# A streaming encoder step: TensorE's order written out by stages as generators, attention staggered by one key tile, x placed tile by tile

## The chip, the cores and the metric

The kernel runs on one core of a Trainium2 chip. A core has five engines, each with its own in-order queue: TensorE (PE, matrix products and transposes through it), VectorE (DVE), ScalarE (ACT), GpSimd (POOL) and SyncE (SP), which here issues all the DMAs. The metric is the device time of one launch in microseconds, the median of three runs.

## The reference, cut to what matters

One layer of a hybrid encoder is applied to a prompt of 2048 tokens (batch 1, no past) and to 64 new tokens of a running stream (the "sample", with 2048 past keys). The model width is 1024.

```python
proj = x @ w_in                       # 1024 x 3856, split among four mixers of 4 heads x 64
o_a  = gated_delta(conv(q, k, v), beta, g)    # recurrence over chunks, triangular solve per chunk
o_b  = stick_breaking(q, k_all, v_all)        # attention; weights below
o_c  = sigmoid(gate) * mlstm(q, k, v, i, f)   # recurrence with a stabiliser
o_d  = hgrn2(silu(q), k, v, log_f)            # recurrence, gate per channel
mix  = (rmsnorm(concat(o_a, o_b, o_c, o_d)) * gates) @ w_out
x    = layernorm(alpha * x + mix)
x    = layernorm(alpha * x + square(relu(x @ w1 + b1)) @ w2 + b2)   # w1: 1024 x 4096

# stick breaking, per head and query block
z     = q @ k.T / 8
log1m = where(kpos < qpos, log_sigmoid(-z), 0)
after = reverse_cumsum(log1m) - log1m         # sum over all later keys
a     = where(kpos < qpos, exp(log_sigmoid(z) + after), 0)
o     = a @ v
```

All is float32. The outputs are y for both sequences, the new keys and values, and the states of the three recurrences.

## The kernel before, in words

**Tiling.** Tokens come in tiles of 128; the sample is one tile of 64. Four tiles make a block (`blocks`; block 0 also holds the sample tile), two tiles a unit (`units`, the piece of a block that the recurrences work on at once). For the MLP the sample tile goes with the last block (`mlps`).

**Products.** Every dense float32 operand is kept as a high and a low part, and `mm3` (L412) makes one product from three matmuls. `load_w` (L387) brings a weight group: at first use the raw weights are loaded, split by ACT (L405) and POOL (L406) and both parts are stored to DRAM; later uses load the parts. Six buffers each hold `whi` and `wlo`. `chan_mm` (L442) puts channels on the partitions (up to 512 tokens wide), `tok_major` (L453) tokens; each result has one of four PSUM buffers (`pd`) until ACT or DVE has taken it away. The transposed x of one block lies in `XH` and `XL` (single buffers). `load_T` (L431) loads a token tile in two halves into `x2` buffers (a ring of six, which the evacuations of the projections use as well) and `split_T` (L423) transposes it by PE, copies the high part by ACT (L428) and the low part by DVE (L429).

**Stages.** `project(b)` (L493) places all tiles of a block, then runs the steps of `w_in` in a list: the queries of attention (`SBQ`), its keys and values (`SBK`, `SBV`), gates, the delta mixer's q, k, v, and so on; results go to DRAM. `ev_k` (L534) also transposes each tile's keys right after the product (L541). `attention(b)` (L1194) goes through the four heads, and for each through the key tiles backwards. A round is two matmuls for the scores (L1217, L1218), a bound by DVE (L1187, or L1190 on the diagonal), exp and ln by ACT (L1167, L1168), the sum of the later tiles added into one row by DVE (L1172), a high part by ACT (L1174) and a low part by POOL (L1175), two matmuls for the sums over keys (L1177, L1178), a subtraction by DVE (L1179), exp (L1180), high part (L1182), low part by DVE (L1183), and the matmuls with the values into `po` (L1224, L1225). Scores and sums share two PSUM buffers (`pa`). `attention_sample` (L1239) does the same for 64 queries over the 16 past key tiles and its own. `gates`, `gdn`, `mlstm` and `hgrn` work a unit off, with one PSUM buffer for the first two (`ps`) and one for the others (`ph`). `mix` (L1353) multiplies the normalised outputs `t.o` by `w_out`, adds x and makes the first layer norm; the result goes to DRAM as `x1`. `mlp(b)` (L1400) runs 16 slices of 256 hidden channels, `up` and one slice later `down` (L1442).

**What sets the order.** The program text goes block by block: `project`, `attention`, the unit's mixers; after the last projection the MLPs. The mixes of the first MLP's tokens stand between the last projection's steps 12 and 16 (`MIX_0`), those of the next MLP's tokens after slices 8 and 12 of the MLP before (`MIX_AT`), and `start` (L1389) places the next MLP's x after its last `up`. A planner then orders the instructions of every engine: it plays the program through with its own costs and lets each engine take, of what is ready, what stands first in the text. So matmuls of attention and recurrences come to lie between those of later projections and MLPs, where the planner thought their operands ready. On the chip each engine follows the planned list in order.

Of the kernel before, what the change touches and what calls it, by code (L numbers as in the profile page):

```python
# [13 lines left out]
P = 128  # L14
# [11 lines left out]
R_X2 = 6  # L26
MIX_AT = (8, 12)
# [26 lines left out]
def encoder_step(ctx: ExitStack, tc: tile.TileContext, a, o):  # L54
# [135 lines left out]
    def move(dst, src):  # L190

        SP.dma_start(dst if dst.dtype == F32 else dst.bitcast(F32), src if src.dtype == F32 else src.bitcast(F32))

# [188 lines left out]

    split = {}
# [47 lines left out]
    def load_T(t, off, src):  # L431

        for g in range(2):
            xt = x2([P, 512])
            SP.dma_start(xt[: t.n], src[:, 512 * g : 512 * g + 512])
            cs = slice(off, off + t.n)
            split_T(xt, t.n, XH[:, 4 * g : 4 * g + 4, cs], XL[:, 4 * g : 4 * g + 4, cs])

# [3 lines left out]
    def chan_mm(gr, b, evac):  # L442
        for o0, n in b.cols:
            pt = pd([P, n])
            for k in range(KD):
                h, l = gr[k // 4]
                mm3(pt, h[:, k % 4, :], l[:, k % 4, :], *x_at(k, slice(o0, o0 + n)), k == 0, k == KD - 1)
            evac(o0, n, pt)

    def chan_major(b, w, c0, evac):  # L450
        chan_mm(chan_w(w, c0), b, evac)
# [18 lines left out]
    pair = [ar([P, 4, 2 * TS], F32R) for _ in range(2)]  # L470

    def natural(b, w, c0, n, evac):
        gr = [load_w(w, 256 * i, 2, c0, n) for i in range(4)]
        for t in b.tiles:
            cs = slice(t.off, t.off + t.n)
            part = []

            def into(pt, first, t=t, part=part):
                if not t.sample:
                    return evac(t, pt)  # L480
                if first:
                    part.append(x2([t.n, n]))
                    return ACT.copy(part[0], pt)
                DVE.tensor_tensor(part[0], part[0], pt, ALU.add)
                evac(t, part[0])
# [7 lines left out]
    def project(b, between={}):  # L493
        for t in b.tiles:
            load_T(t, t.off, t.x)
            if t.sample:
                cs = slice(t.off, t.off + t.n)
                for g in range(2):
                    ACT.copy(pair[g][:, :, 0 : t.n], XH[:, 4 * g : 4 * g + 4, cs].bitcast(F32))
                    POOL.tensor_copy(pair[g][:, :, t.n : 2 * t.n], XL[:, 4 * g : 4 * g + 4, cs].bitcast(F32))  # L500

        def ev_plain(dst, lo=None, hi=None):
# [31 lines left out]
        def ev_k(t, pt):  # L534
# [4 lines left out]
            tp = pd([P, 2, P])  # L539
            for g in range(2):  # L540
                PE.transpose(tp[:, g, : t.n], s[: t.n, g * P : (g + 1) * P], perm if t.n == P else ident[: t.n, : t.n])  # L541
            h = x2([P, 2, P], F32R)
            l = x2([P, 2, P], F32R)
            ACT.copy(h[:, :, : t.n], tp[:, :, : t.n])
            DVE.tensor_tensor(l[:, :, : t.n], tp[:, :, : t.n], h[:, :, : t.n].bitcast(F32), ALU.subtract)

            kk = t.u.kk[:, :, t.j * P : t.j * P + t.n].rearrange("(g i) p n -> i p g n", i=2)
            for i in range(2):
                move(kk[i, rows(i)], h[rows(i), :, : t.n])
                move(kk[i, rows(1 - i)], l[rows(i), :, : t.n])  # L550
# [16 lines left out]
        def nat(c0, n, ev):  # L567
            return [lambda: natural(b, w_in, c0, n, ev)]

        steps = (  # L570
            chan(C_SBQ, 2, ev_q)
            + nat(C_SBK, 256, ev_k)
            + nat(C_SBV, 256, ev_v)
            + nat(C_GATE_A, 264, ev_nat(lambda t: t.ga, 264, True))
# [7 lines left out]
            + nat(C_HGG, 256, ev_nat(lambda t: t.hgg, 256, True))  # L582
        )
        for i, f in enumerate(steps):
            f()
            if i in between:
                between[i]()
# [994 lines left out]
```

## Time and profile before

| | |
|---|---|
| time, median of 3 runs | 3439.55 us (3435.79 to 3444.12) |
| the profiled execution | 3441.77 us, its span 3440.1 us |
| TensorE busy, mean granted clock | 3193.1 us (93%), 0.958 |
| weight loads into TensorE | 2687.6 us (78%) |
| VectorE, ScalarE, GpSimd busy | 2248.2 us, 1355.5 us, 868.0 us |
| DMA moved | 735.66 MB, 214 GB/s on average |

The span runs from the first to the last instruction of one execution. A matmul counts as busy from its start until its result is written; matmuls overlap, so a busy TensorE can still be at half its clock. The granted clock is a share of full speed. In lists of instructions `d<-XH,whi` means that the tile `d` is written from `XH` and `whi`; a group's line ends with the idle time of its engine just before it and what ended that wait.

### The profile page before, as it was taken

Reading aid. Unit: us, or ns where it says so; the run is one execution under the profiler, and the core shown is the slowest. Engines: PE = TensorE matmul, PEld = TensorE weight load, DVE = VectorE, ACT = ScalarE, POOL = GpSimd, SP = SyncE. Lnnn points to the kernel's source line nnn. Section 1 sums busy time; section 2 is a strip of 40 time slices with the busy share of each in tenths; the row PEclk is TensorE's granted clock in tenths of the full one; section 3 lists DMA queues with packets and bytes.
Section 4 is the critical chain, followed back from the end, with each engine's and each line's share of the span. In section 5 each row is a group of like instructions: output and inputs, shape, how many; then the busy total and the mean of one; then the engine's idle time right before and its main releaser. Section 6 shows DMA issues by size and latency. Waiting matters only on the chain. (4 is left out here: it accounts for less than half of the span.)

```text
span 3440.1 us, 60484 instructions
## 1 busy us (share of the span) xinstructions
PE 3193.1 (93%) x20906; PEld 2687.6 (78%) x20906; DVE 2248.2 (65%) x5423; ACT 1355.5 (39%) x3186; POOL 868.0 (25%) x958
## 2 busy tenths in 40 slices
PE   8988898989899888988999899999999999999997
PEld 7987787878787777866877677787777888799986
DVE  2328647565865996788799798779846354564445
ACT  3225434443544455555565545445321111221111
POOL 4322212211222333445454532312201000010001
PEclk9998898999898999998999899999999999999999
DMA  7996565566666776775877675567767587665552
GB/s 231 303 323 183 173 205 188 171 183 202 184 188 203 237 251 219 228 229 169 275 263 255 222 230 180 172 197 219 238 235 260 193 281 243 217 232 165 163 164 81
DMA packets 581614, 735.66 MB, mean 214 GB/s; under 512 B 105864, under 2 KB 310588, under 8 KB 581308
## 3 DMA queue, kind: packets, MB, share of 16 engines
q1 hardware_dynamic: 581308, 731.79, 66.5%
q8 instruction: 166, 2.72, 0.3%
q14 instruction: 140, 1.15, 0.1%
HBM read 548.63 MB, written 182.94 MB: 213 GB/s over the span
## 5 line engine op out<-in xcount | busy, mean ns | idle before, releaser
L413 PE MATMUL d<-XH,whi 128*128 128x512 f32 (+1 forms) x1840 | 666.5, 363 | 11.2 <-DMA whi<-wsp 4.0
L415 PE MATMUL d<-XH,wlo 128*128 128x512 f32 (+1 forms) x1840 | 661.8, 360 | 2.0 <-POOL wlo L406 1.6
L414 PE MATMUL d<-XL,whi 128*128 128x512 f32 (+1 forms) x1840 | 663.0, 360 | 0.1
L1439 DVE TENSOR_TENSOR acc<-d,acc 128x512 f32<-128x512 f32 x564 | 384.9, 686 | 232.5 <-PE d L415 222.0
L413 PE MATMUL d<-whi,hh 128*128 128x512 f32 x992 | 402.6, 407 | 20.0 <-DVE as L1172 6.6
L413 PEld LDWEIGHTS d<-XH,whi 128*128 128x128 f32 x1840 | 351.0, 191 | 61.1 <-DMA whi<-wsp 4.3
L415 PE MATMUL d<-whi,hh 128*128 128x512 f32 x992 | 397.0, 400 | 0.0
L414 PE MATMUL d<-wlo,hh 128*128 128x512 f32 x992 | 395.9, 399 | 0.4 <-DMA wlo<-wsp 0.4
L415 PEld LDWEIGHTS d<-XH,wlo 128*128 128x128 f32 x1840 | 351.1, 191 | 51.4 <-POOL wlo L406 2.3
L1175 POOL TENSOR_TENSOR ar<-as,ar 128x512 fp32r<-128x512 f32 (+3 forms) x177 | 212.5, 1201 | 706.0 <-ACT ar L1174 563.3
L414 PEld LDWEIGHTS d<-XL,whi 128*128 128x128 f32 x1840 | 350.8, 191 | 47.0 <-DVE XL L429 0.4
L406 POOL TENSOR_TENSOR wlo<-raw,whi 128x512 fp32r<-128x512 f32 (+1 forms) x204 | 272.6, 1345 | 327.7 <-ACT whi L405 251.0
L1418 ACT ACTIVATE x<-d,cbig 128x512 f32<-128x512 f32 (+1 forms) x160 | 97.6, 610 | 597.6 <-PE d L415 574.5
L413 PE MATMUL d<-whi,XH 128*128 128x256 f32 (+1 forms) x1024 | 296.8, 298 | 20.7 <-DMA whi<-wsp 7.8
L414 PE MATMUL d<-wlo,XH 128*128 128x256 f32 (+1 forms) x1024 | 298.1, 294 | 5.3 <-POOL wlo L406 4.6
L415 PE MATMUL d<-whi,XL 128*128 128x256 f32 (+1 forms) x1024 | 297.2, 293 | 0.0
L1420 DVE CAST hh<-x 128x512 fp32r<-128x512 f32 (+1 forms) x160 | 75.7, 474 | 259.2 <-ACT x L1419 258.7
L413 PEld LDWEIGHTS d<-whi,hh 128*128 128x128 f32 x992 | 188.8, 190 | 69.3 <-DVE as L1172 8.2
L415 PEld LDWEIGHTS d<-whi,hh 128*128 128x128 f32 x992 | 189.2, 191 | 43.8
L414 PEld LDWEIGHTS d<-wlo,hh 128*128 128x128 f32 x992 | 189.6, 191 | 41.9 <-DMA wlo<-wsp 0.8
L413 PEld LDWEIGHTS d<-whi,XH 128*128 128x128 f32 x1024 | 198.1, 197 | 26.5 <-DMA whi<-wsp 8.5
L414 PEld LDWEIGHTS d<-wlo,XH 128*128 128x128 f32 x1024 | 201.1, 197 | 8.3 <-POOL wlo L406 5.2
(445 smaller groups left out, 6437.9 us busy)
## 6 DMA issues: line engine op xcount, KB each, us to landing
whi<-wsp SPq DMA_DIRECT2D x644, 256.0 KB
wlo<-wsp SPq DMA_DIRECT2D x644, 256.0 KB
wsp<-whi SPq DMA_DIRECT2D x196, 256.0 KB
wsp<-wlo SPq DMA_DIRECT2D x196, 256.0 KB
raw<-in_w_dram SPq DMA_DIRECT2D x128, 256.0 KB
raw<-in_w_in_dram SPq DMA_DIRECT2D x52, 256.0 KB
ak<-kk SPq DMA_DIRECT2D x80, 128.0 KB
ak<-vv SPq DMA_DIRECT2D x80, 128.0 KB
```

What stands on the lines that cost most here:

```text
L406: POOL.tensor_tensor(lo, raw, hi.bitcast(F32), ALU.subtract)
L413: PE.matmul(out, lhsT=lh, rhs=rh, start=start, stop=False)
L414: PE.matmul(out, lhsT=lh, rhs=rl, start=False, stop=False)
L415: PE.matmul(out, lhsT=ll, rhs=rh, start=False, stop=stop)
L1175: POOL.tensor_tensor(sl, sp, sh.bitcast(F32), ALU.subtract)
L1418: ACT.activation(r, pt, AF.Relu, bias=b1c(ff))
L1420: DVE.tensor_copy(h[:, f, cs], r)
L1439: lambda pt, first, acc=acc: DVE.tensor_tensor(acc, pt, acc, ALU.add),
```

## The change: what it does

TensorE's instructions are taken out of the planner's hands (`tc.manual_schedule`): they are issued in the order of the program text, and the text's order is made by generators. The other engines stay with the planner. Every stage (`project`, `gates`, `gdn`, `mlstm`, `hgrn`, both attentions, `mix`, `mlp`, `start`) yields before its next group of matmuls a pair: the TensorE time assumed for the group just issued, and the time assumed until the operands of the next are ready. `interleave` keeps a clock of its own, on which 12 matmuls of n columns are taken as 12 n x 0.00045 us. The dense chain (`dense`: projections, then MLPs, with the mixes inside) runs on; at least every 2.5 us of that clock, or when it has to wait, each of four other chains that is due gets one step: `places` (x into place), `delta` (gates and delta mixer), `memories` (mLSTM, HGRN2) and `attend` (attention). Marks (`flag`, `need`) hold a stage back until what it reads has been issued. Attention issues the next tile's scores right behind a tile's sums, and the tile's value matmuls after the next tile's sums; keys and values of a unit are fetched ahead of use. x is placed tile by tile, the next tile's load issued one tile ahead; a later block's tile goes into place once the last step of the projection before has used that token tile. The projection starts with keys and values, then queries, and the keys' transposes follow one tile later. Beside this: the delta mixer's convolution works on pairs of channel groups; the mixes load the outputs `t.o` by halves ahead of use; `pair` moves from the `ar` ring to the `oh` ring; some POOL memsets (`fill_in`) keep their place in the program's order.

```diff
+MM = 0.00045
+EVERY = 2.5
...
+    def interleave(main, others):
+        due = {id(g): 0.0 for g in [main] + others}
+        alive = [main] + others
+        last = 0.0
+        def step(g):
+            r = next(g, 0)
+            if r is None:
+                return False
+            if r == 0:
+                alive.remove(g)
+            else:
+                clock[0] += r[0]
+                due[id(g)] = clock[0] + r[1]
+            return True
+        while alive:
+            known = len(done)
+            moved = main in alive and due[id(main)] <= clock[0] and step(main)
+            if not moved or clock[0] - last >= EVERY:
+                for g in sorted([g for g in alive if g is not main and due[id(g)] <= clock[0]], key=lambda g: due[id(g)]):
+                    moved = step(g) or moved
+                    last = clock[0]
...
     def chan_mm(gr, b, evac):
...
                 mm3(pt, h[:, k % 4, :], l[:, k % 4, :], *x_at(k, slice(o0, o0 + n)), k == 0, k == KD - 1)
+                if k % 4 == 3 and k < KD - 1:
+                    yield 12 * n * MM, 0
             evac(o0, n, pt)
+            yield 12 * n * MM, 0
...
+    def into_place(b):
+        nxt = load_T(b.tiles[0], b.tiles[0].x)
+        for j, t in enumerate(b.tiles):
+            xt = nxt
+            if b.i:
+                yield from need("xfree", b.i, j)
+            yield from put_T(t, t.off, xt)
+            if j + 1 < len(b.tiles):
+                nxt = load_T(b.tiles[j + 1], b.tiles[j + 1].x)
...
+            flag("xt", b.i, j, after=1.0)
...
         steps = (
-            chan(C_SBQ, 2, ev_q)
-            + nat(C_SBK, 256, ev_k)
+            nat(C_SBK, 256, ev_k, before=lambda t: need("xt", b.i, b.tiles.index(t)))
             + nat(C_SBV, 256, ev_v)
+            + chan(C_SBQ, 2, ev_q)
...
+                yield 0, 4
+                z, carry, prev = scores(*its[0]), None, None
+                pe = 0.5
+                for x, (u, t) in enumerate(its):
+                    zc, sp = stick(z, bound_diag if u.b is b else bound_plain)
+                    sh, sl = add_carry(sp, carry)
+                    yield pe, 7
+                    carry = sums(sh, sl, lowk)
+                    if prev:
+                        add_up(*prev)
+                    if x + 1 < len(its):
+                        z = scores(*its[x + 1])
...
+                    prev = (x, u, t, *weights(zc, carry))
+                    carry = carry[0:1, :]
+                    pe = 1.4
+                yield pe, 4.5
+                add_up(*prev)
...
+    with tc.manual_schedule(engines={PE.engine}):
+        interleave(dense(), [places(), delta(), memories(), attend()])
```

The assumed waits of the other stages have the same form: in `gdn` up to 30 us (the solve's first step), in `hgrn` 25 us (the factors), in `gates` 20 us, else mostly 1.5 to 9 us.

More of the change, by code (lines that the diff above doesn't have):

```diff
@@ L1468, in mlp @@
             elif sb < ns - 1 or not end:
[L1469 to L1473 removed]
+                yield from down([sb - 1])
+            if g:
+                yield from mix(g, ld)
+        yield from down([ns - 2, ns - 1] if end else [ns - 1])
     zero = g2([64, 514])
```

401 lines of the change are left out of this document (269 added, 132 removed).

## The prediction

> **What bounds the kernel now.** I read the page's engine totals and slices first, then the busy time by stretches, then TensorE's waits, then single matmuls in the timeline.
>
> ```profile
> span 3440.1 us, 60484 instructions
> PE 3193.1 (93%) x20906; PEld 2687.6 (78%) x20906; DVE 2248.2 (65%) x5423; ACT 1355.5 (39%) x3186; POOL 868.0 (25%) x958
> ```
>
> TensorE (PE) is the bound, and it loses in two ways: it stands still for 247 us (3440.1 less 3193.1), and for part of its busy time the granted clock is below full. To see where, I cut the span at the points where a block of x is put into place again: the first relu of the first MLP is at 1369 us, and x from x1d is read and waited for at 2555 and 2979 us; the cut between the first two MLPs (1955) is where the matmuls on hh give way to those on XH for good.
>
> ```profile
> L1418 ACT ACTIVATE x<-d,cbig x160: 480/670/693, 1369.2 to 3396.3; 128x512 f32<-128x512 f32 x96, 128x288 f32<-128x288 f32 x64
> 1953.55 0.40 PE L413 MATMUL d<-XH,whi 128*128 128x512 f32 x1
> 2555.22 5.25 DMA x<-x1d
> 2979.28 5.72 DMA x<-x1d
> ```
>
> The busy time by these stretches; the columns are the stretch and its length, the busy time (and count) of PE, of its weight loads, of DVE, ACT and POOL, the granted clock, the DMA engines' share and GB/s:
>
> ```profile
> 0.00:15.00 15.00, 7.65 (x39) 6.44 (x40) 5.47 (x9) 7.51 (x15) 12.83 (x62) 0.96 0.71 213
> 15.00:1365.00 1350.00, 1206.69 (x9411) 1062.97 (x9410) 834.28 (x2427) 586.72 (x1501) 363.93 (x434) 0.93 0.69 215
> 1365.00:1955.00 590.00, 541.00 (x3397) 426.50 (x3397) 495.81 (x1053) 326.07 (x733) 286.40 (x265) 0.96 0.72 232
> 1955.00:2560.00 605.00, 582.91 (x3683) 462.33 (x3681) 472.37 (x1115) 284.64 (x650) 151.59 (x168) 0.99 0.67 213
> 2560.00:2979.00 419.00, 413.85 (x1824) 334.05 (x1822) 204.01 (x353) 70.54 (x125) 26.37 (x14) 1.00 0.73 246
> 2979.00:3410.00 431.00, 428.65 (x2509) 385.75 (x2509) 213.60 (x420) 72.53 (x153) 11.80 (x8) 0.99 0.51 164
> 3410.00:3440.00 30.00, 12.35 (x53) 9.60 (x52) 22.64 (x53) 7.49 (x11) 15.13 (x10) 0.79 0.21 79
> ```
>
> I call a stretch's loss its idle time plus its busy time times the missing clock. The four projections (15 to 1365) lose 143 + 0.07 x 1207 = **228 us**. The first MLP (M0) loses 49 + 0.04 x 541 = 71, the second (M1) 22 + 6 = 28, so **99** together. M2 and M3 lose 5 and 7, the ends some 25. Without any loss the same work would take about 3440 - 228 - 99 - 37 = 3076 us. So the gain to be had lies in the projections, where recurrences and attention run between the dense matmuls. The reader should also see VectorE (DVE): 84% busy in M0 (495.81 of 590), 78% in M1, but 49% in M2, where no side work is left; M2's 204 us is thus what one MLP with its mixes costs DVE alone.
>
> Why the clock drops:
>
> ```profile
> 1816.07 0.75 PE L413 MATMUL d<-whi,hh 128*128 128x512 f32 x1 [0.87 <-DVE as L1187]
> 1816.62 0.63 PE L414 MATMUL d<-wlo,hh 128*128 128x512 f32 x1
> 1817.05 0.63 PE L415 MATMUL d<-whi,hh 128*128 128x512 f32 x1
> 1819.82 0.39 PE L413 MATMUL d<-whi,hh 128*128 128x512 f32 x1
> 1820.05 0.39 PE L414 MATMUL d<-wlo,hh 128*128 128x512 f32 x1
> ```
>
> After a wait of 0.87 us matmuls start 0.43 us apart (1816.62 to 1817.05), and 0.23 apart again by 1819.82: seven or so cost 0.2 us each more, about 1.4 us on top of the wait. Removing waits therefore should give their clock loss back too. The Trainium skill, TensorE: Matmul & The Clock Gate, "What's actually happening", has the clock halved only after an idle window of some 3.4 us. By that, short waits would cost no clock, and the projections' term below would be 0.6 x 143 = 86 rather than 137, the sum 3358. The trace disagrees: the half rate here follows a 0.87 us wait, so the sum counts the clock.
>
> **The change, part by part.** *The fixed order.* No matmul is taken out; each stage hands over a piece with an assumed PE time and an assumed time until its next operand is there, and dense pieces fill the time between. What PE waited for in the projections:
>
> ```profile
> PE po L1224 <- ACT ar L1182: 21.1, 11, 5.8
> PE a L1177 <- ACT ar L1174: 12.3, 8, 3.3
> PE d L413 <- DMA whi<-wsp: 9.1, 3, 6.1
> PE d L413 <- DVE as L1172: 7.5, 5, 2.4
> PE d L427 <- DMA x<-in_x_prompt_dram: 7.5, 4, 2.5
> PE po L1225 <- DVE ar L1183: 6.9, 8, 1.9
> PE d L541 <- DVE x L536: 6.4, 8, 2.1
> PE d L413 <- ACT whi L405: 4.6, 3, 2.5
> PE d L414 <- POOL wlo L406: 4.6, 3, 3.3
> PE h L1114 <- POOL h L1088: 4.1, 1, 4.1
> ```
>
> Of these 84 us, 26 are for weights and x (DMA, L405, L406), which an order cannot remove; 58, about 70%, are operands that ACT, DVE or POOL had not finished. Weights are the early limit: nothing is taken out of their traffic. Take 60% of the stretch's 228 as removed: **-137**. Bounds: 30% (-68), if the assumed times are as often too short as the old order was; 85% (-194), if only the weight waits stay.
>
> *Attention by one key tile.* The next tile's scores go out behind this tile's sums, and the value matmuls one round later, which takes the first and sixth row above off PE. The chain that a round must cover, from scores to the next sums:
>
> ```profile
> L1187 DVE TENSOR_SCALAR as<-a 128x512 f32<-128x512 f32 x96 | 65.5, 682 | 27.7 <-PE a L1218 27.1
> L1167 ACT ACTIVATE as<-as 128x512 f32<-128x512 f32 x112 | 70.5, 630 | 142.3 <-DVE as L1187 130.1 <-POOL g L885 6.0 <-DVE cbig L652 4.4
> L1172 DVE TENSOR_TENSOR as<-as,a 1x512 f32<-1x512 f32 x96 | 65.0, 677 | 15.9 <-ACT as L1168 13.3
> L1174 ACT CAST ar<-as 128x512 fp32r<-128x512 f32 x112 | 69.0, 616 | 44.0 <-DVE as L1172 40.9 <-PE d L414 2.8
> L1175 POOL TENSOR_TENSOR ar<-as,ar 128x512 fp32r<-128x512 f32 x112 | 162.7, 1453 | 440.5 <-ACT ar L1174 335.2 <-PE d L415 30.8 <-issue 15.8
> ```
>
> and the pace so far, by the second sums matmul (L1178), one a round, in the three stretches with attention (busy PE, then weight loads):
>
> ```profile
> 15.00:1365.00 1350.00, 37.10 (x93) 19.05 (x93) 0.93 0.69 215
> 1365.00:1955.00 590.00, 18.63 (x45) 8.71 (x45) 0.96 0.72 232
> 1955.00:2560.00 605.00, 16.03 (x39) 7.45 (x39) 0.99 0.67 213
> ```
>
> 0.68 + 2 x 0.63 (ACT's second pass, L1168, is taken to be as long as the first) + 0.68 + 0.62 + 1.45 = 4.7 us against the 7 assumed: 2.3 us of slack for queueing. A round is 1.4 of PE, 7 of waiting and about 2 until the next look (a dense piece of 12 x 512 columns is 12 x 0.23 = 2.8 us): 10.4 us. M0 had 45 rounds in 590 us, 13.1 each, so the change asks for a faster pace than M0 had.
>
> *Where the side work then falls.* Attention runs block 0 (16 rounds) and the sample's 17 key tiles (some 24 us each by the assumed times) by about 700 us. By the order's own clock, on which nothing waits, the projections end near 15 + 1350 - 228 - 30 = 1110 (the 30 is PE time of rounds that move out; on the chip, with the loss that stays, near 1200). By then 55 prompt rounds are done (16, and some 39 in the 410 us after the sample's), against 93 - 17 = 76 before; 105 instead of 84 stay for the MLPs, and take 105 x 10.4 = 1090 and the heads' ends some 190, to about 2390 of that clock. DVE's side load there grows from 495.81 + 472.37 - 2 x 204 = 560 us to 560 x 105/84 = 700, beside 2.3 x 204 = 470 of dense work, in 1280 us: 91% if PE never waits. Four PSUM buffers cover a late DVE for four pieces of 1.4 us (6 x 0.23) in the second MLP half; beyond that PE stops. The loss there: M0 lost 12% at 84%, M1 4.6% at 78%. The nearest row, 12%, gives 154 of 1280; half of the waits in M0 being operand waits, and 60% of those removed, 108 stay: **+10** against 99. Bounds: -50 (half of the 99 removed) and +165 (the slope between the two rows carried to 91%: 20.6%).
>
> *x tile by tile.* Dense work starts after one tile rather than five, and later blocks are placed while the last projection still runs. PE's wait for these loads:
>
> ```profile
>   DMA x<-in_x_prompt_dram: 20.9, 12
>   DMA x<-x1d: 16.3, 16
> ```
>
> Each of the later loads is issued one tile ahead; the first tile's stays. I take **-10**; bounds 0 and -25. The prefetched halves hold two of the six x2 buffers for as long as PE has not freed the place, and the mixes' o halves two or three more; evacuations of the projections use the same ring, and DVE already waits for it:
>
> ```profile
> L526 DVE TENSOR_SCALAR x<-d 128x256 f32<-128x256 f32 x48 | 20.1, 420 | 44.5 <-PE d L415 19.0 <-DMA vv<-x 15.8 <-DMA ga<-x 6.4
> ```
>
> 22 us of 44.5 here is a buffer still being stored. This lies behind four PSUM buffers: **+4**, bounds 0 and +20. The queue behind such a wait is all of DVE's, thus also the attention's.
>
> *The rest.* SBK and SBV ahead of SBQ, L541's transposes one tile later (counted above), conv groups in pairs (three DMAs, clamps, products and sigmoids instead of six), memsets kept in place: 0, hidden by the dense matmuls that run while a unit's conv waits. Without that cover the clamps tell the size:
>
> ```profile
> L786 DVE TENSOR_SCALAR g<-g 128x256 f32<-128x256 f32 x48 | 16.7, 348 | 0.2
> ```
>
> six of 0.35 us become three of twice the columns, a gain of at most 3 x 0.35 = 1 us a unit.
>
> **Sum:** 3440.1 - 137 + 10 - 10 + 4 = 3307 us span. The profiled execution took 3441.77, 1.7 more than its span, and the median is 2.2 below it: **3307 us**.
>
> **The rivals.** *A, nearly no waits:* all three gains at their good ends, 3440 - 194 - 50 - 25 = 3171. For: the slack of 2.3 us a round. Against: DVE at 91%. *B, DVE becomes the bound in M0 to M2:* 3440 - 137 + 165 - 10 + 4 = 3462; for it the slope between M1 and M0; against it, the slope is two points that differ also in what they held. *C, no change:* the losses only move; the weakest removal, M0's 12% unmended, no gain at x and the ring at 12, 3440 - 68 + 55 + 12 = 3439; DMA at 0.69 busy in the projections speaks a little for it. *D, slower by a rigid order:* PE cannot pass a late operand, and the order was set without regard to DVE's load. If a round really takes M0's 13.1 us where 10.4 are assumed, PE stands 2.7 us in each of the 105 late rounds, 284 us; less the 137, **3587**. It decides from 137/105 = 1.3 us late a round. Against it: the slack above, and a waiting PE unloads DVE. The Trainium skill, TensorE: Matmul & The Clock Gate, step 1 of "What each phase is for", says matmuls stay in program order and only weight loads are pulled ahead; the rows with a wait ahead of L413 agree, and the price is from rows alone.
>
> **How the numbers follow.** Forecast 0.65, A 0.13, B 0.07, C 0.05, D 0.10. About 0.2% (7 us) is what a measurement here tells from no change. Faster: 0.65 + 0.13 = 0.78; same: 0.05; slower: 0.17. The range must hold 8 in 10: from below A, 3160, to just above no change, 3450, which leaves out D, B and a little of A.
>
> **What would show it.** Right: idle and clock loss in the projections fall to about 90 us, the first MLP starts near 1200, the rows po <- ar are gone, L1178 comes every 10 to 11 us of a stretch without loss, and M2's later part and M3 are as before. Wrong: PE waits on a and h tiles in M0 and M1 with DVE over 90%, or the x2 ring holding DVE back.

## The result, and the profile after

The changed kernel takes **3525.45 us** (median of 4 runs, 3518.17 to 3532.68) against 3437.67 for the kernel before beside it: a ratio of 1.0254, 95% interval 1.0225 to 1.0283. It is 2.5% slower, where 3307 us were forecast. The profiled execution took 3528.34 us.

The top of its page:

```profile
span 3526.4 us, 60129 instructions
...
PE 3181.5 (90%) x20906; PEld 2704.2 (77%) x20906; DVE 2239.1 (63%) x5360; ACT 1345.4 (38%) x3048; POOL 841.9 (24%) x946
```

TensorE (PE) is busy about as long as before (3193.1), but the span is 86 us longer: its idle time went from 3440.1 - 3193.1 = 247 to 3526.4 - 3181.5 = 345 us. The other engines have no more work. The stretches, cut like those of before (projections, then the four MLPs), by length, busy PE, weight loads, DVE, ACT, POOL, granted clock, DMA share and GB/s:

```profile
15.00:1290.00 1275.00, 1116.32 (x8563) 1004.66 (x8563) 700.84 (x2057) 463.22 (x1156) 292.12 (x356) 0.92 0.70 219
1290.00:2000.00 710.00, 608.44 (x3957) 485.81 (x3955) 577.38 (x1276) 368.75 (x818) 316.58 (x305) 0.93 0.67 217
2000.00:2645.00 645.00, 593.24 (x3973) 477.41 (x3972) 487.82 (x1160) 316.20 (x707) 148.43 (x179) 0.95 0.60 190
2645.00:3085.00 440.00, 435.63 (x1919) 352.02 (x1918) 244.85 (x419) 113.63 (x201) 43.28 (x28) 1.00 0.74 242
```

With the prediction's measure (idle time plus busy time times the missing clock) the projections lose 159 + 0.08 x 1116 = 248 us (before 228), M0 102 + 43 = 144 (before 71) and M1 52 + 30 = 81 (before 28). The measure counts too much: these three losses together rose by 146 us, the span by 86. Work moved from the projections into the MLPs, as foreseen, and the projections got 75 us shorter; M0 and M1 pay more than that. From the end of M1 on nothing changed: 3526.4 - 2645 = 881 us against 3440.1 - 2560 = 880. DVE is 81% busy in M0 and 76% in M1, less than before (84%, 78%): over a whole stretch it does not set the pace.

What PE waited for, in the view of the waits (total, number, longest), and the value products' groups (busy, mean ns, idle before them):

```profile
PE a L1302 <- ACT ar L1294: 41.2, 20, 6.5
PE m L994 <- DMA g<-wd: 37.8, 16, 17.3
PE m L994 <- POOL g L988: 35.6, 5, 20.4
PE d L478 <- DMA x<-in_x_prompt_dram: 29.9, 13, 4.6
PE a L1303 <- POOL ar L1295: 29.4, 32, 3.6
PE d L464 <- DMA whi<-wsp: 17.6, 12, 4.3
```

```profile
L1363 PE MATMUL po<-ar,ak 128*128 128x512 f32 (+3 forms) x208 | 73.7, 358 | 5.0 <-DVE ar L1313 5.0
L1302 PE MATMUL a<-ar,XH 128*128 128x512 f32 (+3 forms) x177 | 71.9, 406 | 41.3 <-ACT ar L1294 41.2
L1303 PE MATMUL a<-ar,XH 128*128 128x512 f32 (+3 forms) x177 | 71.4, 404 | 29.6 <-POOL ar L1295 29.4
L1362 PE MATMUL po<-ar,ak 128*128 128x512 f32 (+3 forms) x208 | 70.7, 351 | 2.0 <-ACT ar L1312 2.0
L994 PE MATMUL m<-g,g 64*64 64x64 f32 (+1 forms) x528 | 32.2, 272 | 73.6 <-DMA g<-wd 37.8 <-POOL g L988 35.6
```

The waits at the value products are gone (27 + 17 us before, 7 now), which is what the staggering was to do. They came back at the sums (71 us). And there is a wait that the kernel before hardly has (4.3 us): 73.6 us at L994, the first product of the delta stage's triangular solve, for which the order assumes 30 us after the step before it. The longest of them, in the timeline (start, duration, in brackets the idle time before), PE first, then POOL, then the queue of SP:

```profile
1965.11 0.38 PE L1252 MATMUL h<-cbig,h 128*128 128x128 f32 x2
1985.91 0.47 PE L994 MATMUL m<-g,g 64*64 64x64 f32 x2 [20.42 <-POOL g L988]
...
1974.44 3.30 POOL L1660 TENSOR_TENSOR acc<-acc,brd 128x448 f32<-128x448 f32 x2 [1.78 <-ACT acc L1495]
1977.71 3.31 POOL L1661 TENSOR_TENSOR acc<-acc,brd 128x448 f32<-128x448 f32 x2
1982.96 1.70 POOL L1660 TENSOR_TENSOR acc<-acc,brd 128x448 f32<-128x448 f32 x1 [1.94 <-ACT acc L1495]
1984.62 3.64 POOL L988 TENSOR_TENSOR g<-g,cbig 64x256 f32<-64x256 f32 x4
...
1971.76 6.66 SPq L973 DMA_DIRECT2D wd<-g  x14
1979.12 3.68 SPq L980 DMA_DIRECT2D g<-wd  x6
```

PE stands 20.42 us because the next instruction of the written order is the solve's; M0's last group of 12 dense products and the transposes of M1's x stand behind it. The solve's operand goes through DMA stores and loads of `wd` (issued over 6.66 and 3.68 us) and then waits on POOL behind additions of a layer norm (L1660, L1661). These two end the wait, but the longest part of the chain lies ahead of them, on DVE: a substitution (L954 to L966) of 32 short instructions with some 10 us of work. Here it runs from 1936.5 to 1973.0 us, 36.5 us, because DVE does 49 other instructions between. Most of that stretch, and then the same step of the next unit, which took 17.9 us (columns as above):

```profile
1940.00:1973.00 33.00, 22.01 (x277) 17.47 (x275) 32.42 (x79) 14.29 (x33) 5.45 (x4) 0.88 0.35 123
2225.00:2241.00 16.00, 15.99 (x240) 12.73 (x241) 11.48 (x39) 5.76 (x14) 0.32 (x2) 0.81 0.54 163
```

DVE is busy for 32.42 of 33 us in the first. Of the five units in which PE waits 6 us or more for the solve's first product, the step takes 30 to 37 us in four and 19.6 in one; in the other four it takes 13 to 18. So the waits that the view puts down to DMA and POOL were mostly made in DVE's queue; no run frees DVE to show it by itself. The order's clock knows none of these queues.

### The profile page after: what moved, and what is told of

Its sections match the earlier page's. It is cut to its first block, busy times and chain, and to the rows that moved or that the text cites. A ratio compares the mean times of both kernels' runs of the same rounds, so it can differ in the third digit from the quotient of the medians.

```text
span 3526.4 us, 60129 instructions
## 1 busy us (share of the span) xinstructions
PE 3181.5 (90%) x20906; PEld 2704.2 (77%) x20906; DVE 2239.1 (63%) x5360; ACT 1345.4 (38%) x3048; POOL 841.9 (24%) x946
## 4 chain that ended last, share of the span: by engine, by line
PE 59%; DVE 17%; DMA 11%; SPq 4%; issue 4%; ACT 3%; POOL 2%; POOLq 0%; DVEq 0%; ACTq 0%
PE d L464 16%; PE d L465 16%; PE d L466 16%; DMA wlo<-wsp 1%; SPq L195 1%; DVE acc L1639 1%; DMA g<-qkv 1%; DMA vv<-x 1%; PE d L527 1%; PE a L1303 1%; DMA x<-in_x_prompt_dram 1%; DVE acc L1564 1%; DVE g L959 1%; POOL ar L1295 1%; DVE g L884 1%
## 5 line engine op out<-in xcount | busy, mean ns | idle before, releaser
L464 PE MATMUL d<-XH,whi 128*128 128x512 f32 (+1 forms) x1840 | 675.6, 367 | 3.7 <-ACT whi L456 3.0
L465 PE MATMUL d<-XL,whi 128*128 128x512 f32 (+1 forms) x1840 | 661.0, 359 | 1.0 <-DVE XL L480 0.9
L1295 POOL TENSOR_TENSOR ar<-as,ar 128x512 fp32r<-128x512 f32 (+3 forms) x177 | 198.2, 1120 | 956.5 <-ACT ar L1294 840.0
L464 PE MATMUL d<-whi,hh 128*128 128x512 f32 x992 | 404.9, 408 | 12.6 <-ACT x L1618 4.2
L465 PE MATMUL d<-wlo,hh 128*128 128x512 f32 x992 | 396.2, 399 | 0.1
L464 PEld LDWEIGHTS d<-XH,whi 128*128 128x128 f32 x1840 | 352.4, 192 | 53.7 <-ACT whi L456 3.2
L465 PEld LDWEIGHTS d<-XL,whi 128*128 128x128 f32 x1840 | 352.2, 191 | 46.6 <-DVE XL L480 1.4
L464 PE MATMUL d<-whi,XH 128*128 128x256 f32 (+1 forms) x1024 | 316.3, 309 | 26.3 <-DMA whi<-wsp 15.4
L465 PE MATMUL d<-wlo,XH 128*128 128x256 f32 (+1 forms) x1024 | 307.9, 301 | 11.9 <-DMA wlo<-wsp 8.1
L466 PE MATMUL d<-whi,XL 128*128 128x256 f32 (+1 forms) x1024 | 305.3, 298 | 2.6 <-DVE XL L480 2.6
L464 PEld LDWEIGHTS d<-whi,XH 128*128 128x128 f32 x1024 | 211.6, 207 | 32.5 <-DMA whi<-wsp 17.4
L464 PEld LDWEIGHTS d<-whi,hh 128*128 128x128 f32 x992 | 190.0, 192 | 57.2 <-ACT x L1618 5.1
L465 PEld LDWEIGHTS d<-wlo,XH 128*128 128x128 f32 x1024 | 211.3, 206 | 17.1 <-DMA wlo<-wsp 11.5
L465 PEld LDWEIGHTS d<-wlo,hh 128*128 128x128 f32 x992 | 190.0, 192 | 41.2 <-DMA wlo<-wsp 0.8
```

The source lines that it names most:

```text
L464: PE.matmul(out, lhsT=lh, rhs=rh, start=start, stop=False)
L465: PE.matmul(out, lhsT=lh, rhs=rl, start=False, stop=False)
L466: PE.matmul(out, lhsT=ll, rhs=rh, start=False, stop=stop)
L1295: POOL.tensor_tensor(sl, sp, sh.bitcast(F32), ALU.subtract)
```

## The experiments

All ratios are to the kernel before, run in the same group (medians 3437 to 3444 us). The kernels, with span, busy PE and granted clock of the profiled execution:

| run | us | ratio (95%) | span - busy = idle | clock |
|---|---|---|---|---|
| changed kernel | 3525.45 | 1.0254 (1.0225-1.0283) | 3526.4 - 3181.5 = 345 | 0.946 |
| after_w3 | 3526.78 | 1.0249 (1.0232-1.0266) | 3530.3 - 3186.7 = 344 | 0.943 |
| planner_w3 | 3423.05 | 0.9951 (0.9933-0.9968) | 3422.2 - 3182.8 = 239 | 0.959 |
| solve50 | 3470.34 | 1.0082 (1.0056-1.0107) | 3468.5 - 3165.6 = 303 | 0.951 |
| att10 | 3677.49 | 1.0692 (1.0661-1.0723) | 3673.9 - 3233.5 = 440 | 0.921 |
| deep | 3443.17 | 1.0005 (0.9992-1.0017) | 3438.6 - 3145.6 = 293 | 0.958 |
| deep_ring6 | 3455.74 | 1.0048 (1.0030-1.0066) | 3448.4 - 3154.9 = 294 | 0.954 |
| xfirst | 3529.71 | 1.0256 (1.0232-1.0281) | 3517.8 - 3177.2 = 341 | 0.947 |
| solve50_xall | 3492.91 | 1.0142 (1.0111-1.0173) | 3485.4 - 3179.0 = 306 | 0.948 |
| planner_xall | 3393.33 | 0.9865 (0.9845-0.9885) | 3383.5 - 3160.2 = 223 | 0.965 |
| planner_flat | 3377.73 | 0.9805 (0.9789-0.9821) | 3376.2 - 3173.2 = 203 | 0.965 |
| planner_deep | 3368.47 | 0.9781 (0.9758-0.9804) | 3366.1 - 3143.6 = 223 | 0.967 |
| planner_coarse | 3537.78 | 1.0292 (1.0269-1.0315) | 3538.7 - 3251.5 = 287 | 0.931 |
| after_unpinned | 3521.70 | 1.0244 (1.0229-1.0259) | 3519.0 - 3171.7 = 347 | 0.949 |
| coarse_unpinned | 3512.04 | 1.0208 (1.0190-1.0226) | 3511.8 - 3222.2 = 290 | 0.945 |
| flat_single | 3382.82 | 0.9832 (0.9806-0.9858) | 3382.8 - 3168.2 = 215 | 0.961 |
| coarse_single | 3545.07 | 1.0301 (1.0269-1.0334) | 3550.8 - 3251.1 = 300 | 0.930 |

### Is it the order, or the rest of the text?

**planner_w3** gives PE back to the planner and leaves the text as it is:

```diff
-W_RAW, W_SP = 4, 6
+W_RAW, W_SP = 3, 6
-    with tc.manual_schedule(engines={PE.engine}):
-        interleave(dense(), [places(), delta(), memories(), attend()])
+    interleave(dense(), [places(), delta(), memories(), attend()])
```

> The changed text (stages as generators, staggered attention, x tile by tile) without the hand-fixed order: the planner of the kernel before orders TensorE again; the ring of raw weights has 3 buffers instead of 4, for room. Theory T1 (the fixed order stands at operands that come later than it assumes: 73 us at the solve's first product, 71 us at the attention's sums, and the clock lost behind them): these waits go and the time falls to 3380 to 3450. Rival R1 (the rest of the text is at fault: the later attention, the rings, the x tiles): it stays at 3500 or above.

**after_w3** is the control: the changed kernel with the first two lines of that edit alone.

> The changed kernel with 3 buffers instead of 4 for raw weights, which the run under the planner needed for room. If the ring doesn't matter: 3515 to 3540, and the planner's run differs from the changed kernel by its order alone. If a shorter ring holds the weights back: over 3545, and the planner's gain is larger than measured; under 3510, and part of it was the ring.

The control takes 3526.78 us; the ring does nothing. Under the planner the same text takes 3423.05, so the fixed order alone costs 104 us, and the changed text without it is 0.5% faster than the kernel before. R1 is out. The groups of planner_w3 that answer to those above:

```profile
L1302 PE MATMUL a<-ar,XH 128*128 128x512 f32 (+3 forms) x177 | 71.2, 402 | 13.9 <-ACT ar L1294 12.3 <-DVE x L612 1.1 <-DVE XL L480 0.4
L1303 PE MATMUL a<-ar,XH 128*128 128x512 f32 (+3 forms) x177 | 68.2, 385 | 2.9 <-POOL ar L1295 2.8
...
L994 PE MATMUL m<-g,g 64*64 64x64 f32 (+1 forms) x528 | 27.3, 241 | 3.9 <-DMA g<-wd 3.3 <-ACT g L1011 0.4
```

73.6 us at the solve became 3.9, and 71 at the sums 17; 36 us of waits at the value products are back.

### Which assumed times are too short?

**solve50** changes one number of the fixed order:

```diff
-            yield (0.9, 30) if bs == 16 else (0.8, 2.5)
+            yield (0.9, 50) if bs == 16 else (0.8, 2.5)
```

> The changed kernel with one number changed: behind the product after which the solve starts, the order assumes that its operand is there 50 us later, not 30. T1: the 73 us at the solve's first product shrink to under 25, and with the clock behind them 50 to 90 us are won: 3435 to 3475. Rival R2 (the solve's wait only stands in for the next one, since what bounds those stretches is VectorE or the chain of the delta stage): the waits move to the products that follow and the time stays within 3505 to 3560.

It wins 55 us. The wait at the solve is gone, and the solve's matmuls, no longer run on a PE that has just stood still, take 220 ns instead of 272. Not all of the 74 us is won: PE's idle time falls by 42 us and its busy time by 16, while other operands are waited for longer (x 36 us instead of 30, the sums 80 instead of 71):

```profile
L1302 PE MATMUL a<-ar,XH 128*128 128x512 f32 (+3 forms) x177 | 72.0, 407 | 47.1 <-ACT ar L1294 44.5 <-DVE cbig L1121 1.1 <-DVE h L1126 0.9
L1303 PE MATMUL a<-ar,XH 128*128 128x512 f32 (+3 forms) x177 | 71.6, 405 | 32.5 <-POOL ar L1295 29.7 <-DVE cbig L1122 2.7
L994 PE MATMUL m<-g,g 64*64 64x64 f32 (+1 forms) x528 | 18.8, 220 | 0.0
```

**att10** does the same for the attention:

```diff
-                    yield pe, 7
+                    yield pe, 10
```

> The changed kernel with one number changed: the attention's assumed time from scores to sums 10 us instead of 7. T1: the waits at the two sums, 41 and 29 us, shrink to under 20 together, and 40 to 70 us are won: 3455 to 3485. Rival R3 (with 10 us a tile the side chain gets longer than the dense work it is laid between, and the last mixes or the MLP wait for it): 3525 or above, with a late attention in the last stretches.

It is 152 us slower than the changed kernel: T1's simple reading fails and R3 holds. With 10 us a round the chain of attention, one round after the other, ends at 2995 us instead of 2812, and the dense products that could lie between run out at 2800. Windows of att10 (columns as above), and one round of its timeline there:

```profile
2700.00:2800.00 100.00, 100.00 (x446) 81.54 (x445) 48.30 (x88) 30.27 (x56) 7.40 (x7) 1.00 0.62 198
2800.00:2900.00 100.00, 45.26 (x99) 25.70 (x97) 35.38 (x61) 41.05 (x72) 14.90 (x13) 0.53 0.14 42
2900.00:3000.00 100.00, 46.88 (x92) 26.23 (x93) 34.01 (x52) 40.66 (x66) 16.54 (x13) 0.50 0.07 20
```

```profile
2825.49 0.63 PE L1353 MATMUL a<-aq,ak 128*128 128x512 f32 x1
2829.70 0.80 PE L1302 MATMUL a<-ar,XH 128*128 128x512 f32 x1 [3.58 <-ACT ar L1294]
2831.10 0.80 PE L1303 MATMUL a<-ar,XH 128*128 128x512 f32 x1 [0.60 <-POOL ar L1295]
...
2837.19 0.80 PE L1302 MATMUL a<-ar,XH 128*128 128x512 f32 x1 [3.58 <-ACT ar L1294]
```

200 us with PE less than half busy and DMA nearly still: all that PE issues here are rounds of attention, since the next mix is written behind the end of the attention that it needs. This stretch also measures the attention's chain by itself. From the end of the scores (2825.49 + 0.63) to the second sums (2831.10) it takes 5.0 us, and a round 7.49. The prediction's 4.7 us was nearly right for an empty machine. In the changed kernel the last operand of the sums, POOL's low part, is done 6.2, 8.0 and 6.7 us after the scores (medians in the projections, M0 and M1), and in a quarter of the rounds only after 8.2, 10.2 and 9.0 us: 1 to 3 us of queueing in the median round, on engines that have other work, where 2.3 us of slack were left. The sums themselves are issued 9.3, 9.5 and 9.0 us after the scores, which is what 7 assumed and the next look some 2 us later make, so PE stands only in the late rounds, 29 of these 144. Waiting longer in the order is no remedy, since the chain has 160 rounds to get through.

**deep** shortens the chain instead. On top of solve50 it issues each tile's scores one round earlier:

```diff
+                ready, carry, prev = [], None, None
+                def ahead(x):
+                    if x < len(its):
+                        u, t = its[x]
+                        if u not in kv:
+                            kv[u] = fetch(u)
+                        ready.append(stick(scores(u, t), bound_diag if u.b is b else bound_plain))
+                ahead(0)
+                ahead(1)
...
-                    zc, sp = stick(z, bound_diag if u.b is b else bound_plain)
+                    zc, sp = ready.pop(0)
...
-                        z = scores(*its[x + 1])
+                    ahead(x + 2)
```

> The run with the solve's assumed 50 us, and beside it the attention's scores issued one key tile earlier, so that scaling, exponential and logarithm of a tile lie before the sums of the tile ahead of it, not between two sums. Buffers as in the changed kernel. Theory T2 (the 74 us at the sums that were left come from a chain of 9 to 10 us a tile, of which the order assumes 7): the chain between two sums gets shorter than 7 us, the two rows at the sums fall under 25 us together, and the time to 3395 to 3430. Rival R4 (what is late at the sums is the queue of VectorE and ScalarE in front of them, whatever lies in the chain, or the four buffers hold the earlier scores back): the rows keep over 50 us and the time stays at 3450 or above.

**deep_ring6** is the same with `R_AS` 6 instead of 4 and `W_RAW` 3 instead of 4.

> As the run before it, with six buffers instead of four for the attention's scores, and three instead of four for raw weights to make room. If the four buffers hold the earlier scores back, this one is 10 to 30 us faster than that run; if not, within 10 us of it.

deep takes 3443.17 us, 27 less than solve50, and is level with the kernel before (the interval includes 1). The sums:

```profile
L1302 PE MATMUL a<-ar,XH 128*128 128x512 f32 (+3 forms) x177 | 69.9, 395 | 4.4 <-DVE acc L1571 2.3 <-ACT ar L1294 2.1
L1303 PE MATMUL a<-ar,XH 128*128 128x512 f32 (+3 forms) x177 | 66.8, 377 | 17.7 <-POOL ar L1295 17.7
```

80 us became 22, as T2 has it, but only 27 of the expected 40 to 75 us arrived, and PE's idle time fell by just 10 us. The rest went into other late operands: PE waits 39.0 us for x (L478), 36 for split weights (L464 and L465) and 18 at the value products, against 35.6, 28 and 6 in solve50. Six buffers are 13 us slower, outside both bands, so the four were not the brake.

### x tile by tile

**xfirst** places the first block's x whole before its first product:

```diff
-before=lambda t: need("xt", b.i, b.tiles.index(t)))
+before=lambda t: need("xt", b.i, b.tiles.index(t) if b.i else len(b.tiles) - 1))
```

> The changed kernel with the first block's x tiles all placed ahead of its first dense product, as in the kernel before; later blocks tile by tile. If the x tiles, whose loads stand behind weight stores on SP, are what costs the start its 30 us of waits and the half rate behind them, 15 to 30 us are won: 3495 to 3510. If the loads are late in any case, the start only waits elsewhere: 3520 to 3535.

The time does not move (1.0256 against 1.0254). That lies in the second band, but not for its reason: the loads did come sooner. In the changed kernel PE waits for the tiles one by one:

```profile
23.41 1.11 PE L478 MATMUL d<-cbig,x 128*128 128x128 f32 x4 [4.15 <-DMA x<-in_x_prompt_dram]
33.36 1.08 PE L478 MATMUL d<-cbig,x 128*128 128x128 f32 x4 [3.12 <-DMA x<-in_x_prompt_dram]
42.28 0.43 PE L478 MATMUL d<-cbig,x 64*128 64x64 f32 x4 [3.49 <-DMA x<-in_x_sample_dram]
```

In xfirst no wait there is longer than 1.76 us after the first, and the last tile is placed from 23.49 us on instead of 42.28. Windows of the changed kernel, then of xfirst, with the wait that stands out in the second of them:

```profile
0.00:100.00 100.00, 65.14 (x397) 60.59 (x397) 19.64 (x43) 24.02 (x54) 31.60 (x78) 0.85 0.68 214
100.00:290.00 190.00, 182.35 (x1356) 178.17 (x1357) 118.66 (x341) 79.19 (x179) 75.14 (x72) 0.96 0.90 289
```

```profile
0.00:100.00 100.00, 76.07 (x510) 70.91 (x510) 22.36 (x52) 27.97 (x62) 37.09 (x83) 0.93 0.73 226
100.00:290.00 190.00, 170.04 (x1236) 165.79 (x1237) 110.90 (x331) 76.73 (x172) 68.85 (x67) 0.93 0.88 284
...
PE m L927 <- DVE g L912: 13.4, 1, 13.4
```

Tile by tile does cost the start: 65 us of busy PE in the first 100, against 76 with x placed whole and 84 in the kernel before. But what xfirst wins there it loses in the next 190 us, at one product of the delta stage (L927, 13.4 us), which the order now reaches before its operand. An earlier start only brings the next late operand forward.

**solve50_xall** does it for every block on top of solve50, **planner_xall** on top of planner_w3:

```diff
-before=lambda t: need("xt", b.i, b.tiles.index(t)))
+before=lambda t: need("xt", b.i, len(b.tiles) - 1))
```

> The run with the solve's assumed 50 us under the fixed order, with every block's x placed whole before its first product. Its waits at the x loads were 36 us, all in the stretches of the projections. If tile by tile placement costs in this order what it costs under the planner (30 us): 3430 to 3450. If the waits only come in one piece instead of several, or what follows is bound by the weights' loads (DMA 88 to 90% busy behind the start): 3460 to 3480.

> The run under the planner (raw weights in 3 buffers) with every block's x placed whole before its first dense product, as in the kernel before. If the x tile by tile is what the planner's run gained on the kernel before, it falls back to 3433 to 3445; if it's the attention's order or the rest of the text, it stays within 3415 to 3430.

The signs differ. Under the fixed order x whole is 23 us slower than solve50; under the planner it is 30 us faster than planner_w3, where 3433 to 3445 was expected if x was the gain and 3415 to 3430 if not. So x tile by tile is a loss under the planner and a gain of about the same size under the fixed order. Both expectations were missed, on opposite sides. In solve50_xall the waits for x did fall, from 36 to 24 us, but those for split weights (L464) rose from 16 to 27; why the two orders differ was not shown.

### What is left under the planner

**planner_deep** adds deep's edit to planner_xall. **planner_flat** puts the attention's text of the kernel before into planner_xall: scores, sums and value products of a tile one behind the other, with one yield a tile:

```diff
+                for x, (u, t) in enumerate(its):
+                    if u not in kv:
+                        kv[u] = fetch(u)
+                    zc, sp = stick(scores(u, t), bound_diag if u.b is b else bound_plain)
+                    carry = sums(*add_carry(sp, carry), lowk)
+                    add_up(x, u, t, *weights(zc, carry))
+                    carry = carry[0:1, :]
+                    yield 1.4, 7
```

> The planner's run with every x whole, and the attention's scores one key tile earlier still (the edit of the run with the earlier scores). Under the fixed order it won 27 us. If it is the chain that is late, whoever orders TensorE: the rows at the value products and the sums (60 us) halve and the time is 3350 to 3385. If the planner already lays other work into that time, or the chain's queue is what is late: within 3385 to 3400; above that, the earlier scores hold buffers that others want.

> The planner's run with every x whole, with the attention's text as in the kernel before: scores, sums and value products of one key tile one behind the other. If the pipelining by one key tile is what makes that run 47 us faster than the kernel before, it goes back to 3425 to 3445; if the rest of the text does it (the pairs of channels in the delta stage, the order of the first products), it stays at 3385 to 3405.

3368 and 3378 us; their intervals overlap. Staggering by two tiles and none at all do equally well, and staggering by one (3393) is 16 to 25 us worse. planner_flat misses both its bands on the fast side. So under the planner staggering is not where the gain is. In planner_deep the rows at the value products and sums did not halve either (57 us against 60 in planner_xall), and PE's idle time is the same 223 us; it is in the expected band, but not for the reason given there. planner_deep beats both kernels: 2.2% faster than the one before.

**planner_coarse** asks where it is then. It is planner_flat with the text in the order of the kernel before:

```diff
-    interleave(dense(), [places(), delta(), memories(), attend()])
+    for b in blocks:
+        run(into_place(b))
+        run(project(b, dict(zip(MIX_0, mlps[0].groups)) if last else {}))
+        run(attention(b))
...
+        for u in b.units:
+            for stage in (gates, gdn, mlstm, hgrn):
+                run(stage(u))
...
+    for m in mlps:
+        run(start(m))
+        run(mlp(m))
```

> The planner's run with the attention's text as before, and now with the whole text in the order of the kernel before: a block's placement, its projections, its attention, then its units' delta, mLSTM and HGRN stages, each written out to its end, none laid between the others; x whole. What is left of the change are the pairs of channels, the order of the first products, the later transposes and the buffers. If the planner, which takes the text's order into account, gains from the finely interleaved text, this run loses most of the 62 us that the run with interleaved text and flat attention has on the kernel before: 3420 to 3450. If the edits inside the stages are what gains: 3370 to 3390.

3537.78 us, far outside both bands: 160 more than planner_flat, which differs by nothing but the order of the text. The planner takes what stands first among what it holds ready; that the interleaved text thereby gives the recurrences and the attention their turn in time is the likely reason, but it was not tested further. The stretch of planner_coarse with the lowest clock, and the same time in planner_flat:

```profile
900.00:1200.00 300.00, 244.52 (x1784) 208.03 (x1782) 184.88 (x530) 127.81 (x337) 86.17 (x116) 0.74 0.48 148
900.00:1200.00 300.00, 273.54 (x1988) 230.86 (x1988) 220.29 (x569) 133.41 (x318) 97.19 (x100) 0.95 0.80 261
```

No single wait carries that loss. The longest row of planner_coarse is the one at HGRN's product, and its longest wait lies elsewhere, at 607 us:

```profile
PE h L1231 <- POOL h L1202: 28.6, 10, 11.1
```

But planner_coarse is also 100 us slower than the kernel before, which neither theory has. Two of the changed edits were tried for it: the memsets that the change pins in the text's order on POOL, and the pairs of channels in the delta stage.

```diff
-        tc.keep_in_program_order(POOL.memset(dst, v))
+        POOL.memset(dst, v)
```

after_unpinned is after_w3 with this edit, coarse_unpinned is planner_coarse with it and `R_X2` 5 instead of 6.

> The changed kernel with 3 buffers for raw weights and with its memsets on GpSimd free to move. If the pinned memsets are what makes GpSimd late at the solve, the row of the solve behind GpSimd (41 us in the run with 3 buffers) falls under 15 and the time by 20 to 40 us, to 3485 to 3507. If GpSimd is late for its other work (the additions, the differences), the row stays over 25 and the time within 3515 to 3540.

> The run with the text in the order of the kernel before, with the memsets free to move, and 5 buffers instead of 6 in the ring of the projections' evacuations, for room. If the pinned memsets hold the later stages back where their text stands behind a whole block, the wait of the HGRN products behind GpSimd (29 us) goes and the time falls to 3430 to 3470. If it is something else, 3515 or above.

**flat_single** and **coarse_single** put the convolution per channel (six loads, clamps and products, one-row buffers) into planner_flat and planner_coarse.

> The planner's run with flat attention (x whole, raw weights in 3 buffers), with the delta stage's convolution per channel as in the kernel before, six loads and clamps instead of three. If the pairs cost or gain nothing, as the prediction had it: 3370 to 3386. If they gain by fewer instructions: 3390 or more. If they hold buffers: 3365 or less.

> The run with the text in the order of the kernel before, with the convolution per channel. If the pairs' buffers are what makes it slower than the kernel before: 3440 to 3480. If not: 3525 to 3550, and what is left of its loss stays open.

The pinned memsets are not what holds POOL at the solve. With them free the row stays:

```profile
PE m L994 <- DMA g<-wd: 36.1, 16, 14.8
...
PE m L994 <- POOL g L988: 31.6, 4, 16.7
```

and the time, 1.0244, too. In the coarse text the two edits together win 26 us, and the wait at HGRN's product leaves the list, but the time did not fall into either band. The pairs change nothing that can be measured (1.0292 and 1.0301 coarse, 0.9805 and 0.9832 interleaved; all intervals overlap). What makes the remaining 75 us between coarse_unpinned and the kernel before was not found; the two also differ in the places of `start`, in the buffers, in the products' order and in the later transposes of the keys.

## Why the prediction was wrong, by its own steps

**What bounds the kernel: right.** PE's idle time and the clock behind it are what can be won; the times of the table go with the two together. planner_deep's span is 74 us shorter than before, by 24 us less idle time and 50 us less busy time for the same 20906 matmuls at a clock of 0.967 instead of 0.958.

**Projections, -137: the step that failed.** It took 58 of 84 us of waits to be operands that an order can bring in time, and removed 60% of the stretch's loss without pricing the new order's own waits. The loss became 248, not 90, and the first MLP started at 1290 us, not near 1200. A written order removes a wait only where its assumed time is at least what the chip takes under load. For the solve it assumes 30 us; the first product came 36 to 58 us after the transposes before it, and 50 us assumed took the wait away and 55 us off the run. The prediction gave this 30 us no row and no bound, though the trace of before had both: there the planner let 27 to 65 us pass (DVE's substitution alone took 12 to 43), and the group of the solve's first products cost almost no idle time:

```profile
L890 PE MATMUL m<-g,g 64*64 64x64 f32 (+1 forms) x528 | 23.9, 229 | 4.3 <-ACT g L905 2.0 <-DMA g<-wd 1.1 <-POOL g L885 0.7
```

Some 50 us less 30 for each of the nine units, up to 180 us of late operands, is the term that should have stood in the sum with a plus; 74 us of waits and 55 us of time were measured. Of the 104 us that the fixed order costs, 55 are the solve's by solve50. Deep's 27 can't be booked to the order, since the same edit wins 25 under the planner (3393.33 to 3368.47). About half of the 104 us stays open; waits for x and for split weights are the largest rows left in deep.

**Attention, 4.7 us against 7: the chain right, the queueing mis-sized.** Alone the chain measures 5.0 us; among the other stages 6 to 8 in the median round and 8 to 10 or more in a quarter of them. The rows po <- ar went, as forecast, but the stall went to the sums (71 us), and a round of M0 came every 710 / 49 = 14.5 us, not 10 to 11 (its second sums, by number):

```profile
1290.00:2000.00 710.00, 20.52 (x49) 9.55 (x49) 0.93 0.67 217
```

Deep's 27 us is what a shorter chain won back.

**MLP stretches, +10: wrong.** M0 and M1 lose 225 us against 99, +126, near the upper bound (+165) but for another reason. DVE at 81% and 76% is below the 91% forecast, so DVE is not the bound that rival B has, and no group of PE's waits for DVE is among the six largest. But its queue, which the prediction put behind the x2 ring and the attention alone, drew the solve's substitution out to 30 us and more, and in a fixed order PE stood for it. More side work moved there, as worked out, and PE stood at its operands.

**x tile by tile, -10: wrong in sign for the start** (65 us busy in the first 100 instead of 84: the later tiles' loads are issued one tile ahead, and PE waited 4.15, 3.12 and 3.49 us for them), hidden by the next late operand. For all blocks together, placing tile by tile is worth 23 us under the fixed order (solve50) and costs 30 under the planner. **x2 ring, +4:** no row of PE's waits points to it; but DVE's waits for its buffers to be stored did grow, from about 55 us to 74. How much of that reached PE was not tried.

**The rest, 0: right for the pairs, wrong for the text.** Two runs show nothing measurable from the pairs. What was overlooked is that the same generators also reorder the text which orders the other engines and which a planner reads: worth 160 us between planner_coarse and planner_flat.

**The clock.** The sum counted clock loss behind short waits. In att10's lone attention the waits are 3.58 us and the granted clock 0.50 to 0.53. The Trainium skill, TensorE: Matmul & The Clock Gate, "What's actually happening", has the clock halved after an idle window of about 3.4 us, which agrees there. The row of 0.87 us that the prediction showed is shorter, but it does not stand alone: in the ten us before it PE also waited 1.15 and 0.58 us. No run here shows what a single short wait costs.

**Rivals.** D was the right one in its mechanism: PE can't pass a late operand. Neither part of its price, 3587, came true: the old waits' 137 us were not won, and the attention's rounds did not cost 284. It put the whole of the lateness at these rounds, and half of it was at the solve. PE's 71 us at the sums are 0.4 us for each of 177 rounds, below its point of decision of 1.3; with the solve's 74 they are 0.8.

## What to carry to other kernels

A hand-written order is a table of assumed times, and each is a term of the sum: price it against the interval that the profile of before shows for the same pair of instructions under load, not against the sum of the chain's durations, and with every queue that lies between. Look ahead of the engine that ends a wait, too: here DMA and POOL ended it, and DVE's queue had made it. A late operand on a fixed order stops everything behind it, and assuming more time is only free while the chain it belongs to has time left, so shorten the chain first. Try the reordered text with the planner left in charge: here the finely interleaved text was worth having and freezing it cost 104 us.

## What the runs showed that was not expected

- In the changed kernel the first 32 small matmuls of a solve take 317 to 321 ns each where PE had stood 3 us or more before them; in solve50, where it never had, those of every full unit take 221. Over all 528 the means are 272 and 220; they overlap, and all of them together keep PE busy for 32.2 against 18.8 us. A stall ahead of a short stream costs that stream part of its rate, beside its own length.
- With 10 us assumed instead of 7, PE spent 200 us at less than half busy with DMA at 14% and 7%: a side chain that is late does not cost where it is late, but where the dense work runs out.
- One and the same edit, x placed whole, costs 23 us under one way of ordering and wins 30 under the other.
